# The 16 low-rank gate columns as one 32-column stationary operand

## The chip, the cores and the metric

One Trainium2 chip, one core. The metric is the device time of one execution in microseconds (us). Engines are called by their names in the profile: PE is TensorE, DVE is VectorE, ACT is ScalarE, POOL is GpSimd, SP issues most of the loads.

## What is computed

One layer of a hybrid decoder for 256 positions of width 2048, in float32: a mixer of three branches (S5, GLA, HGRN2) with a gated merge, then a squared-ReLU MLP, each followed by a layer norm. All branches read one projection `h = x @ w_in`, whose columns are split among them. The change concerns 16 of these columns, the low-rank input of GLA's decay gate:

```python
h = x @ w_in                                   # x 256 x 2048, w_in 2048 x 14352
(u_a, q_b, k_b, v_b, glow_b, gate_b, ...) = split_columns(h)      # glow_b: 16 columns

# GLA branch: per-key decay from the low-rank columns
log_a = log_sigmoid(glow_b @ w_gate + b_gate) / 16                # w_gate 16 x 512
o = chunk_gated_linear_attention(q_b * 128 ** -0.5, k_b, v_b, log_a)
```

## The kernel before

**Products in parts.** Weights and activations are float32. So that TensorE can run them in its faster 32-bit type (`F32R`), each is split into an upper part `hi` (a copy into F32R) and a lower part `lo` (the remainder), and products are summed without the lower-by-lower one. The columns of `x` are kept transposed as tiles `a` with 128 rows of the inner dimension, `a[0]` upper, `a[1]` lower (256 positions each), and `a[2]` both side by side (512 columns).

**Chunks and steps.** All weight matrices are worked off as a list of `Chunk`s. A chunk's weights come in pages of 512 KB, loaded on SP's queue 8 pages ahead (`fetch`, `emit_dma`) and split by ACT (`hi`, line 184) and DVE (`lo`, line 188) up to 6 steps ahead (`emit_split`, `emit_lower`). One pass of the loop at line 1288 is one step: half of a page's products. There are three kinds of chunk:

- "rows" (512 weight columns as the moving operand, activations stationary): three products of 512 columns for each 128 rows of the inner dimension, lines 1327 to 1329.
- "cols" (256 weight columns, 128 at a time as the stationary operand): for each 128 rows a product of 512 moving columns with `hi` against `a[2]` (line 1332) and one of 256 with `lo` against `a[0]` (line 1333), called a pair here. The result has two halves, which `joined` adds (ACT copies one, DVE adds it to the other).
- "low": one chunk alone, for the 16 low-rank columns. It is like "cols", with 128 weight columns of which only the first 16 are wanted: 2 pages, 4 steps, 16 pairs. Its evacuation `ev_low` (line 760) adds the two halves of 16 rows into `glT` and spawns `gla_decay`.

The order is: a "rows" chunk of v (16 steps), four "cols" chunks of the S5 input u (32 steps, 0 to 47 with v's), the "low" chunk (steps 48 to 51), two "cols" chunks for gK, two for gQ, and so on; then the other branches, the merge, the output projection and the MLP.

**Tasks.** Work that isn't a chunk's products runs as generators in `tasks`: at each step `run_tasks` advances those that are due. `yield n` makes a task due 2n steps later. Tasks of priority -1 always run; others only while an estimate of the work handed to DVE and ACT (`used`, reduced by 1240 ns each a step) is below zero, in order of priority. The S5 branch (`s5_params`, `s5_prepare`, `s5_main`) runs at priority 2 and 5 beside the chunks up to about 760 us: `s5_prepare` transposes blocks of S5 matrices on TensorE (lines 440 to 442), `s5_main` computes tables on POOL (lines 484 to 489), scans on DVE and small products on TensorE (lines 510 and 554). `gla_decay` (line 768, priority 0) loads the gate's weights on ACT's queue, multiplies (line 779, plain float32) and computes the decay `gA`; `gla` waits for `gA`, gQ and gK before it starts its attention.

Each engine works through its instructions in program order. Tiles of 512 KB ("pg", 41 of them) and of 256 KB ("hf", 18) are handed out and freed by the program; PSUM has three accumulators for chunks ("acc"), three tiles for tasks ("m") and two for S5 ("m2").

Of the kernel before, what the change touches and what calls it, by code (L numbers as in the profile page):

```python
# [8 lines left out]
F32 = mybir.dt.float32  # L9
F32R = mybir.dt.float32r  # L10
U8 = mybir.dt.uint8
AF = mybir.ActivationFunctionType
ALU = mybir.AluOpType
# [14 lines left out]
C_UA, C_QB, C_KB, C_VB, C_GL, C_GB = 0, 1024, 1536, 2048, 3072, 3088  # L28
# [8 lines left out]


class Chunk:

# [12 lines left out]
def trunk_kernel(ctx: ExitStack, tc, io, out):  # L56
    nc = tc.nc
    V, S, G, T = nc.vector, nc.scalar, nc.gpsimd, nc.tensor
# [25 lines left out]
    def half(shape=(128, 2, 256), dt=F32):  # L84
        return take("hf", shape, dt)

    def free(*tiles):
        for t in tiles:
            tag = "pg" if id(t) in live["pg"] else "hf"
            del live[tag][id(t)]  # L90

    def psm(shape=(128, 512)):
        uid[0] += 1
        return psa.tile(list(shape), F32, tag="m", bufs=NM, name=f"m{uid[0]}")
# [10 lines left out]
    def tt(o, a, b, op):  # L105
        used["v"] += size(o) / 0.96 + 80
        V.tensor_tensor(o, a, b, op=op)  # L107
# [12 lines left out]
    def act(o, a, f, bias=None, scale=None, accum=None):  # L120
        used["s"] += size(a) / 1.3 + 180
        kw = {}
        if bias is not None:
            kw["bias"] = bias
        if scale is not None:
            kw["scale"] = scale
        if accum is not None:
            kw["accum_out"] = accum
        S.activation(o, a, f, **kw)  # L129
# [11 lines left out]
    w_in = io["w_in"][0]  # L141
# [5 lines left out]
    chunks = []  # L147
# [53 lines left out]
    def spawn(gen, prio):  # L201
        tasks.append([prio, now[0], gen, len(tasks)])
        tasks.sort(key=lambda x: (x[0], x[3]))
# [529 lines left out]
    def ev_page(key, i, func=None, scale=None):  # L733

        def f(t, ps):
            n = 2 * i + t
            if n == 0:
                R[key] = page()
            o = R[key][:, n, :]
            joined(ps, o, scale)  # L740

            def later():
                yield 0.5
                if func is not None:
                    act(o, o, func)
                if n == 3:
                    yield 0.5
                    R[key, "ok"] = True
            spawn(later(), -1)
        return f  # L750
# [6 lines left out]
        while not all(k in R for k in keys):  # L757
            yield 1

    def ev_low(t, ps):  # L760

        glT, b = half((16, 256)), half((16, 256))
        act(b, ps[0:16, 256:512], AF.Copy)
        tt(glT, ps[0:16, 0:256], b, ALU.add)
        free(b)
        spawn(gla_decay(glT), 0)

    def gla_decay(glT):

        wg = half((16, 512))  # L770
        S.dma_start(wg, io["gla_w_gate"][0])
        yield 2
        A = page()
        L = page()
        for hp in range(2):
            ps = psm()
            for i in range(2):
                hd = 2 * hp + i
                T.matmul(ps[:, i * 256:(i + 1) * 256], lhsT=wg[:, hd * 128:(hd + 1) * 128], rhs=glT,
                         start=True, stop=True)  # L780
            for i in range(2):
                hd = 2 * hp + i
                act(A[:, hd, :], ps[:, i * 256:(i + 1) * 256], AF.Identity, bias=S5["bgate"][:, hd:hd + 1])
        free(wg, glT)
        yield
        act(L, A, AF.Abs)
        act(L, L, AF.Exp, scale=-1.0)
        yield 0
        act(L, L, AF.Ln, bias=1.0)
        stt(A, A, 0.0, L, ALU.min, ALU.subtract)  # L790
        yield
        act(A, A, AF.Exp, scale=1.0 / 16.0)
        free(L)
        R["gA"] = A

    def gla():
        yield from wait_for("gA", ("gQ", "ok"), ("gK", "ok"))
        nw = half((128, 256))
        S.dma_start(nw, io["gla_norm_w"].to_broadcast([128, 256]))
        ss = cst.tile([128, 2, 4], F32, name="gss")  # L800

        def sink(t, g, ps):
            y = R["gg", g][:, t, :]
            y3 = y.rearrange("p (h d) -> p h d", h=2)
            tt(y3, y3, nw.unsqueeze(1).to_broadcast([128, 2, 256]), ALU.mult)
            squares(ss[:, t, 2 * g:2 * g + 2], [ps[:, i * 256:(i + 1) * 256] for i in range(2)])
            tt(y, ps, y, ALU.mult)
            yield 0
        yield from attention(R["gQ"], R["gK"], R["gA"], [("gv", "ok"), ("gg", "ok")],
                             lambda t, h: R["gv", h // 2][:, t, (h % 2) * 256:(h % 2) * 256 + 256], 256, sink)  # L810
        free(nw)
        yield from rms(ss.rearrange("p a b -> p (a b)"), 256)
        for t in range(2):
            for h in range(4):
                y = R["gg", h // 2][:, t, (h % 2) * 256:(h % 2) * 256 + 256]
                ts(y, y, ss[:, t, h:h + 1], None, ALU.mult)
            yield 0
        free(R["gv", 0], R["gv", 1])
        R["yB"] = True
# [244 lines left out]
    xact = parts(xq)  # L1064
# [13 lines left out]
    def four(w, c0, ev):  # L1078
        return [col_chunk(w, D, c0 + 256 * i, xact, ev(i)) for i in range(2)]
# [18 lines left out]
    def at(chunk, f):  # L1098
        hooks.setdefault(id(chunk), []).append(f)
# [4 lines left out]
    v_chunk(0)  # L1104
    for c in range(2):
        four(w_in, C_UA + c * 512, lambda i: ev_u(c, i))
    chunks.append(Chunk([w_in[:, C_GL:C_GL + 128].rearrange("(kt p) n -> p kt n", p=128)], xact, ev_low, "low"))
    at(four(w_in, C_KB, lambda i: ev_page("gK", i))[0], lambda: spawn(gla(), 0))
    four(w_in, C_QB, lambda i: ev_page("gQ", i, scale=128 ** -0.5))
    v_chunk(1)  # L1110
    for c in range(2):
# [160 lines left out]
    def accumulator():  # L1272
        tags = [("acc", NACC)] * NACC + ([("m2", 2)] * 2 if "done" in S5 else [])
        tag, bufs = tags[acc_n[0] % len(tags)]
        acc_n[0] += 1
        uid[0] += 1
        return psa.tile([128, 512], F32, tag=tag, bufs=bufs, name=f"acc{uid[0]}")
# [10 lines left out]
    for s, (c, ku, j, t) in enumerate(steps):  # L1288
        now[0] = s
        if id(c) not in started:  # L1290
            started.add(id(c))
            for f in hooks.get(id(c), []):
                f()
        old = split_n[0]
        early = ln_from - 8 <= s < ln_from + 12
        kept = max(0, 8 - len(x1q)) if early and s >= ln_from else 0
        while (split_n[0] < len(order) and first_use[split_n[0]] <= s + (14 if early else 2 if s < 14 else LA + 4 * (s > 660))
               and len(live["pg"]) + 2 + kept <= limit["pg"]):
            emit_split()
        if early:  # L1300
            emit_lower(split_n[0])
        evacuate()
        fetch()
        run_tasks(1240, 1240)
        emit_lower(old if s >= 10 else split_n[0])
        if s < 14 and t == 1:
            x_piece(s // 2 + 1)
        k = c.index[ku, j]
        if k not in sps:
            emit_split()  # L1310
        emit_lower(k + 1)
        hi, lo = sps[k]
        kpu = c.kpu
        nk = len(c.units) * kpu
        if t not in c.ps:
            c.ps[t] = c.ps[0] if c.kind == "low" and t else accumulator()
        ps = c.ps[t]
        nj = kpu // 2
        wn = c.units[0].shape[2]
        wh, wl = (a.rearrange("p a b -> p (a b)").rearrange("p (k n) -> p k n", n=wn) for a in (hi, lo))  # L1320
        for i in range(nj):
            kt = ku * kpu + j * nj + i
            f, l = kt == 0, kt == nk - 1
            a = c.act(kt)
            if c.kind == "rows":
                sl = slice(t * 128, (t + 1) * 128)
                T.matmul(ps, lhsT=a[0][:, sl], rhs=wh[:, i, :], start=f, stop=False)  # L1327
                T.matmul(ps, lhsT=a[0][:, sl], rhs=wl[:, i, :], start=False, stop=False)  # L1328
                T.matmul(ps, lhsT=a[1][:, sl], rhs=wh[:, i, :], start=False, stop=l)  # L1329
            elif c.kind == "cols" or i // (nj // 2) == t:  # L1330
                n = slice(t * 128, (t + 1) * 128) if c.kind == "cols" else slice(0, 128)
                T.matmul(ps, lhsT=wh[:, i, n], rhs=a[2], start=f, stop=False)  # L1332
                T.matmul(ps[:, 0:256], lhsT=wl[:, i, n], rhs=a[0], start=False, stop=l)  # L1333
        uses_left[k] -= 1
        if uses_left[k] == 0:
            free(*sps.pop(k))
        if ku == len(c.units) - 1 and j == 1 and (c.kind != "low" or t == 1):
            done.append((c, t, ps))
    evacuate()
    guard = 0  # L1340
# [53 lines left out]
```

## Time and profile before

| | |
|---|---|
| median of 3 runs | 1694.68 us (1694.48 to 1695.0) |
| profiled execution | 1694.67 us, span 1692.9 us |
| PE busy | 1669.5 us (99%) |
| DVE busy | 1196.9 us (71%) |
| ACT busy | 826.0 us (49%) |
| POOL busy | 166.3 us (10%) |
| read from HBM | 308.71 MB |

The span is that of the recorded instructions; the execution's own time has 1.8 us more around it. PE's busy time counts products whose ends are modelled and overlap, so the distance between the starts of two products tells the pace, not the length of one. In lines of instructions the columns are start in us, length in us, engine, line of the kernel, operation, output and inputs, count, and in brackets the engine's idle time before and what ended it. PEld is the weight load, which runs beside products. Helpers record their line: L129 is every ACT activation, L107 every DVE operation on two tensors, L134 every transpose.

### The profile page before, as it was taken

Reading aid. Unit: us, or ns where it says so; the run is one execution under the profiler, and the core shown is the slowest. Engines: PE = TensorE matmul, PEld = TensorE weight load, DVE = VectorE, ACT = ScalarE, POOL = GpSimd, SP = SyncE. Lnnn points to the kernel's source line nnn. Section 1 sums busy time; section 2 is a strip of 40 time slices with the busy share of each in tenths; the row PEclk is TensorE's granted clock in tenths of the full one; section 3 lists DMA queues with packets and bytes.
Section 4 is the critical chain, followed back from the end, with each engine's and each line's share of the span. In section 5 each row is a group of like instructions: output and inputs, shape, how many; then the busy total and the mean of one; then the engine's idle time right before and its main releaser. Section 6 shows DMA issues by size and latency. Waiting matters only on the chain.

```text
span 1692.9 us, 24205 instructions
## 1 busy us (share of the span) xinstructions
PE 1669.5 (99%) x9390; PEld 1385.6 (82%) x9390; DVE 1196.9 (71%) x1586; ACT 826.0 (49%) x1166; POOL 166.3 (10%) x121
## 2 busy tenths in 40 slices
PE   8999999999999999999999999999999999999996
PEld 6888888887877877878888888888888888888885
DVE  5978889698999999985675667555455555555556
ACT  4463554464545444435554466454454545454540
POOL 3132211021322322100000000000000000000000
PEclk9999999999999999999999999999999999999998
DMA  9855565555555665766686555656656565656661
GB/s 289 255 160 170 166 178 173 159 166 163 173 179 150 222 188 165 244 199 196 189 278 210 171 162 157 196 178 191 199 187 210 168 207 166 219 173 203 205 216 50
DMA packets 222899, 318.70 MB, mean 188 GB/s; under 512 B 13204, under 2 KB 122128, under 8 KB 222784
## 3 DMA queue, kind: packets, MB, share of 16 engines
q1 hardware_dynamic: 218448, 309.45, 58.6%
q10 hardware_dynamic: 3568, 6.46, 1.3%
q0 software_dynamic: 768, 1.25, 0.5%
q8 instruction: 74, 1.21, 0.3%
q14 instruction: 41, 0.34, 0.1%
HBM read 308.71 MB, written 2.10 MB: 184 GB/s over the span
## 4 chain that ended last, share of the span: by engine, by line
PE 91%; DVE 5%; ACT 1%; DMA 1%; issue 1%; SPq 0%; DVEq 0%; ACTq 0%
PE acc L1332 21%; PE acc L1327 19%; PE acc L1328 19%; PE acc L1329 19%; PE acc L1333 10%; DVE pg L107 2%; DMA pg<-in_w_in_dram 1%; DVE hf L107 1%; PE m L554 1%; ACT pg L129 1%; PE m L134 1%; DVE pg L118 1%; ACT hf L129 1%; PE m L625 1%; PE pb L510 0%
## 5 line engine op out<-in xcount | busy, mean ns | idle before, releaser
L129 ACT ACTIVATE pg<-pg 128x1024 fp32r<-128x1024 f32 (+2 forms) x604 | 603.4, 1028 | 416.5 <-DVE pg L107 131.9
L107 DVE TENSOR_TENSOR pg<-pg,pg 128x1024 fp32r<-128x1024 f32 (+3 forms) x646 | 752.5, 1192 | 65.4 <-ACT pg L129 39.5
L1327 PE MATMUL acc<-pg,pg 128*128 128x512 f32 x1504 | 595.4, 396 | 4.2 <-ACT pg L129 3.6
L1328 PE MATMUL acc<-pg,pg 128*128 128x512 f32 x1504 | 587.7, 391 | 1.1 <-DVE pg L107 1.1
L1329 PE MATMUL acc<-pg,pg 128*128 128x512 f32 x1504 | 587.2, 390 | 0.3 <-DVE pg L107 0.2
L1332 PE MATMUL acc<-pg,pg 128*128 128x512 f32 x1552 | 551.2, 400 | 0.0
L1333 PE MATMUL acc<-pg,pg 128*128 128x256 f32 x1552 | 436.2, 281 | 0.0
L1332 PEld LDWEIGHTS acc<-pg,pg 128*128 128x128 f32 x1552 | 292.2, 188 | 72.4 <-issue 0.7
L1327 PEld LDWEIGHTS acc<-pg,pg 128*128 128x128 f32 x1504 | 282.9, 188 | 68.2 <-issue 5.4
L1329 PEld LDWEIGHTS acc<-pg,pg 128*128 128x128 f32 x1504 | 282.7, 188 | 61.1 <-DVE pg L107 1.1
L1328 PEld LDWEIGHTS acc<-pg,pg 128*128 128x128 f32 x1504 | 283.1, 188 | 59.5 <-DVE pg L107 4.0
L1333 PEld LDWEIGHTS acc<-pg,pg 128*128 128x128 f32 x1552 | 293.9, 189 | 0.7 <-DVE pg L107 0.2
L129 ACT ACTIVATE hf<-acc 128x256 f32<-128x256 f32 (+2 forms) x103 | 39.9, 387 | 186.1 <-PE acc L1333 177.7
L107 DVE TENSOR_TENSOR pg<-pg,acc 128x512 f32<-128x512 f32 x56 | 38.3, 684 | 123.0 <-PE acc L1329 123.0
L107 DVE TENSOR_TENSOR hf<-acc,hf 128x256 f32<-128x256 f32 (+1 forms) x69 | 29.1, 421 | 134.6 <-ACT hf L129 134.6
L107 DVE TENSOR_TENSOR hf<-hf,hf 128x512 f32<-128x512 f32 (+1 forms) x144 | 117.3, 833 | 3.5 <-ACT hf L129 1.4
L129 ACT ACTIVATE hf<-hf 128x256 f32<-128x256 f32 (+1 forms) x152 | 67.7, 455 | 2.1 <-DMA hf<-pg 0.2
L129 ACT ACTIVATE pg<-acc 128x512 f32<-128x512 f32 x40 | 23.8, 594 | 77.9 <-PE acc L1329 77.8
L107 DVE TENSOR_TENSOR hf<-pb,hf 128x256 f32<-128x256 f32 x128 | 46.4, 414 | 19.1 <-PE pb L510 13.3
L107 DVE TENSOR_TENSOR pg<-hf,pg 128x256 fp32r<-128x256 f32 x84 | 34.7, 422 | 27.7 <-ACT pg L129 27.6
L129 ACT ACTIVATE pg<-m 128x512 fp32r<-128x512 f32 (+2 forms) x35 | 19.7, 562 | 66.2 <-PE m L134 47.1
L484 POOL TENSOR_TENSOR hf<-pg 128x512 f32<-128x512 f32 x16 | 19.8, 1238 | 303.4 <-PE pb L510 85.9
(127 smaller groups left out, 665.9 us busy)
## 6 DMA issues: line engine op xcount, KB each, us to landing
pg<-in_w_in_dram SPq DMA_DIRECT2D x224, 512.0 KB, 4.2
pg<-in_w_mlp_in_dram SPq DMA_DIRECT2D x128, 512.0 KB, 4.6
pg<-in_w_mlp_out_dram SPq DMA_DIRECT2D x128, 512.0 KB, 4.1
pg<-in_w_up_dram SPq DMA_DIRECT2D x48, 512.0 KB, 4.7
pg<-in_w_out_dram SPq DMA_DIRECT2D x32, 512.0 KB, 5.1
pg<-in_s_w_glu_dram SPq DMA_DIRECT2D x8, 512.0 KB, 4.8
hf<-pg SPq DMA_DIRECT2D x96, 32.0 KB, 2.1
hf<-hf SPq DMA_DIRECT2D x96, 32.0 KB, 1.9
```

The lines of the kernel that those rows point to most:

```text
L107: V.tensor_tensor(o, a, b, op=op)
L118: V.scalar_tensor_tensor(o, a, s, b, op0=op0, op1=op1)
L129: S.activation(o, a, f, **kw)
L134: T.transpose(ps[:, i * 128:(i + 1) * 128], s, ident)
L484: G.tensor_tensor(co, coarse(cs), fine(cs), op=ALU.mult)
L554: T.matmul(yps[r, 0:256], lhsT=W[:, 2 + ri, r], rhs=m[:, i, :], start=ri == 0, stop=ri == 1)
L625: T.matmul(ps[32 * c:32 * c + 32, i * 16:(i + 1) * 16], lhsT=Kf[:, r], rhs=q4[:, :, 1, :], start=True, stop=True)
L1327: T.matmul(ps, lhsT=a[0][:, sl], rhs=wh[:, i, :], start=f, stop=False)
L1328: T.matmul(ps, lhsT=a[0][:, sl], rhs=wl[:, i, :], start=False, stop=False)
L1329: T.matmul(ps, lhsT=a[1][:, sl], rhs=wh[:, i, :], start=False, stop=l)
L1332: T.matmul(ps, lhsT=wh[:, i, n], rhs=a[2], start=f, stop=False)
L1333: T.matmul(ps[:, 0:256], lhsT=wl[:, i, n], rhs=a[0], start=False, stop=l)
```

## The change

The "low" chunk goes. A task `low_rank` of priority -1, spawned when gK's first chunk starts, loads only the 16 columns (64 bytes of each of 2048 rows) on POOL's queue, splits them into one tile with the upper part in columns 0 to 15 and the lower part in columns 16 to 31, and multiplies with that as a 32-column stationary operand against `a[2]`: 16 products of 512 moving columns. The 32 rows of the result are added over the two halves to `glT` with 32 rows, and the gate's weights are loaded twice, one copy below the other, so that the gate's product sums the upper and lower part.

```diff
-    def ev_low(t, ps):
-
-        glT, b = half((16, 256)), half((16, 256))
-        act(b, ps[0:16, 256:512], AF.Copy)
-        tt(glT, ps[0:16, 0:256], b, ALU.add)
-        free(b)
+    def low_rank():
+        wgr, wgl = half((128, 16, 16)), half((128, 16, 32), F32R)
+        G.dma_start(wgr, w_in[:, C_GL:C_GL + 16].rearrange("(kt p) n -> p kt n", p=128))
+        yield 4
+        act(wgl[:, :, 0:16], wgr, AF.Copy)
+        yield 0.5
+        tt(wgl[:, :, 16:32], wgr, wgl[:, :, 0:16].bitcast(F32), ALU.subtract)
+        yield 1
+        ps = psm()
+        for kt in range(16):
+            T.matmul(ps[0:32, :], lhsT=wgl[:, kt, :], rhs=xact(kt)[2], start=kt == 0, stop=kt == 15)
+        glT, b = half((32, 256)), half((32, 256))
+        act(b, ps[0:32, 256:512], AF.Copy)
+        yield 0.5
+        tt(glT, ps[0:32, 0:256], b, ALU.add)
+        free(b, wgr, wgl)
         spawn(gla_decay(glT), 0)
 
     def gla_decay(glT):
 
-        wg = half((16, 512))
-        S.dma_start(wg, io["gla_w_gate"][0])
+        wg = half((32, 512))
+        for i in range(2):
+            S.dma_start(wg[16 * i:16 * i + 16], io["gla_w_gate"][0])
...
-    chunks.append(Chunk([w_in[:, C_GL:C_GL + 128].rearrange("(kt p) n -> p kt n", p=128)], xact, ev_low, "low"))
-    at(four(w_in, C_KB, lambda i: ev_page("gK", i))[0], lambda: spawn(gla(), 0))
+    kb = four(w_in, C_KB, lambda i: ev_page("gK", i))
+    at(kb[0], lambda: spawn(gla(), 0))
+    at(kb[0], lambda: spawn(low_rank(), -1))
...
-            c.ps[t] = c.ps[0] if c.kind == "low" and t else accumulator()
+            c.ps[t] = accumulator()
...
-            elif c.kind == "cols" or i // (nj // 2) == t:
-                n = slice(t * 128, (t + 1) * 128) if c.kind == "cols" else slice(0, 128)
+            else:
+                n = slice(t * 128, (t + 1) * 128)
...
-        if ku == len(c.units) - 1 and j == 1 and (c.kind != "low" or t == 1):
+        if ku == len(c.units) - 1 and j == 1:
```

## The prediction

> **What bounds the kernel now.** I read the page first, then the stretches around the change, then the instructions themselves in order of time. The head of the page:
>
> ```profile
> span 1692.9 us, 24205 instructions
> PE 1669.5 (99%) x9390; PEld 1385.6 (82%) x9390; DVE 1196.9 (71%) x1586; ACT 826.0 (49%) x1166; POOL 166.3 (10%) x121
> PE 91%; DVE 5%; ACT 1%; DMA 1%; issue 1%; SPq 0%; DVEq 0%; ACTq 0%
> ```
>
> TensorE (PE) is busy for 99% of the span and carries 91% of the chain that ended last. So TensorE work that disappears comes off the time, unless something else is late at that place. The low-rank work lies near 85 to 91 us. From the table of stretches the row of 85 to 96 us (busy us of PE, PEld, DVE, ACT, POOL, then granted clock, DMA share, GB/s), the low-rank products in order of time on TensorE, and ScalarE's evacuations at both ends:
>
> ```profile
> 85.00:96.00 11.00, 8.98 (x51) 7.33 (x50) 10.95 (x14) 3.52 (x6) 7.51 (x6) 0.98 0.26 80
> 85.22 0.28 PE L1333 MATMUL acc<-pg,pg 128*128 128x256 f32 x1
> 85.34 0.40 PE L1332 MATMUL acc<-pg,pg 128*128 128x512 f32 x1
> ...
> 90.99 0.40 PE L1332 MATMUL acc<-pg,pg 128*128 128x512 f32 x1
> 85.54 0.38 ACT L129 ACTIVATE hf<-acc 128x256 f32<-128x256 f32 x1
> ...
> 91.19 0.38 ACT L129 ACTIVATE hf<-acc 16x256 f32<-16x256 f32 x1 [3.37 <-PE acc L1333]
> ```
>
> The 16-partition evacuation at 91.19 is that of the low-rank chunk, the 128-partition one at 85.54 that of the chunk before. So the chunk's 16 pairs of products run from 85.34 to 90.99, gap-free, one pair per 0.353 us. Behind them comes a wait:
>
> ```profile
> 92.38 0.28 PE L1333 MATMUL acc<-pg,pg 128*128 128x256 f32 x1
> 93.75 0.44 PE L134 MATMUL m<-ident,s5eb 128*128 128x128 f32 x2 [1.09 <-DVE s5eb L435]
> 95.12 0.44 PE L134 MATMUL m<-ident,s5ec 128*128 128x128 f32 x2 [0.94 <-DVE s5ec L112]
> ```
>
> Here TensorE waits for VectorE (DVE), which is busy for 10.95 of 11 us, as it prepares the S5 operands.
>
> **The change part by part.** *Products removed.* 16 pairs, 90.99 - 85.34 = 5.65 us, all on TensorE's path.
>
> *Products added.* 16 products with a 32-column stationary operand and 512 moving columns, none of which the trace has in this form. Rows that come near: 512-column products back to back with 128 stationary columns, and 32-column stationary operands in plain f32 (output of the S5 branch), two interleaved column groups of four products each:
>
> ```profile
> 745.42 0.39 PE L1327 MATMUL acc<-pg,pg 128*128 128x512 f32 x1
> ...
> 746.10 0.39 PE L1327 MATMUL acc<-pg,pg 128*128 128x512 f32 x1
> 206.46 0.39 PE L1329 MATMUL acc<-pg,pg 128*128 128x512 f32 x1
> 206.77 1.06 PE L554 MATMUL m<-hf,hf 128*32 128x256 f32 x8
> 207.77 0.50 PE L1327 MATMUL acc<-pg,pg 128*128 128x512 f32 x1
> L554 PEld LDWEIGHTS m<-hf,hf x128: 106/110/110, 146.2 to 756.9; 128*32 128x32 f32 x128
> L554 PE MATMUL m<-hf,hf x128: 379/379/404, 146.2 to 757.1; 128*32 128x256 f32 x128
> ```
>
> The first rows are three products apart, (746.10 - 745.42)/3 = 0.227 us per 512 columns. I take that: 16 x 0.227 = 3.63 us. The 32-column rows give the same pace: from first to last of one group's four products, (1.06 - 0.379)/3 = 0.227 us. The weight loads of 0.110 us do not add to it, so they are hidden behind the product before. Going from 128- to 32-column operands costs 206.77 - 206.46 = 0.31 us instead of 0.227, and about the same on the way back (207.83 - 0.379 = 207.45 to 207.77): 0.08 us each, 0.16 us together. Ends: 3.63 us without the two changes; 16 x (0.227 + 0.110) + 0.16 = 5.55 us if every weight load shows. Near the lower end, because the nearest form (32 columns) hides its loads. Taken: 3.8 us.
>
> *The position.* The new products stand at step 59 (spawned at 48, then 8 + 1 + 2 steps of yields), inside the gK chunks. The wait at 93 us stays: the S5 transposes are emitted at step 53 by yields that nothing removed here feeds, and five steps of 1.41 us stand in front of them from 85.34 on in either kernel. Until then VectorE has the same splits to do, one page per two steps in either. Cost 0.
>
> *Splits and loads removed.* Two 512 KB loads on SP's queue, two page splits on ScalarE (ACT) and VectorE:
>
> ```profile
> L129 ACT ACTIVATE pg<-pg 128x1024 fp32r<-128x1024 f32 x569 | 584.4, 1054 | 392.9 <-DVE pg L107 124.7 <-PE acc L1328 119.9 <-PE acc L1329 96.5
> L107 DVE TENSOR_TENSOR pg<-pg,pg 128x1024 fp32r<-128x1024 f32 x569 | 700.8, 1255 | 39.1 <-ACT pg L129 33.8 <-PE acc L1328 2.9 <-issue 0.9
> L129 ACT ACTIVATE hf<-hf 128x256 f32<-128x256 f32 x120 | 49.4, 412 | 1.9
> L107 DVE TENSOR_TENSOR hf<-acc,hf 128x256 f32<-128x256 f32 x68 | 28.6, 421 | 134.6 <-ACT hf L129 134.6
> L771 ACTq DMA_DIRECT2D hf<-in_gla_w_gate_dram x1: 397/397/397, 91.2 to 91.2; - x1
> 108.70 0.42 DVE L107 TENSOR_TENSOR pg<-acc,hf 128x256 f32<-128x256 f32 x1 [7.64 <-ACT hf L129]
> ```
>
> ScalarE loses 2 x 1.05 and gains 0.41 (first part of the 256-element split) and 0.40 (issue of the second gate-weight load); VectorE loses 2 x 1.26 and gains 0.42. None of it is on the path: the new evacuations replace equal ones. I count nothing for 1.7 us of VectorE work saved, because VectorE then idles 7.64 us before 108.70 and carries no debt onwards. In the other direction the cover of the new split is three steps (56 to 59, about 4 us), against 0.41 + 0.42 us of work; without it TensorE would wait those 0.8 us.
>
> *Chain behind it.* The gate decay starts at step 60 instead of 52. Its readers wait for gQ as well, whose chunks end at step 80, twenty steps later. No wait is added there.
>
> *The new load.* It is issued from POOL's queue, 2048 runs of 64 bytes. In program order it stands ahead of the S5 tables (priority -1 at step 48; the tables follow at 51), and only 11 of the 18 half tiles were handed out before, so it need not wait for a buffer. POOL idles from 16.3 us. So it goes out at about 16.3 us, into the crowded start:
>
> ```profile
> 10.04 1.71 POOL L291 DMA_DIRECT2D pg<-in_s_b_re_dram  x1 [0.18 <-issue]
> 11.74 1.69 POOL L292 DMA_DIRECT2D pg<-in_s_b_im_dram  x1
> 15.72 0.55 POOL L587 DMA_DIRECT2D dg<-in_c_diag_dram  x1
> 79.49 1.43 POOL L484 TENSOR_TENSOR hf<-pg 128x512 f32<-128x512 f32 x1 [63.23 <-DVE pg L114]
> pg<-in_w_in_dram SPq DMA_DIRECT2D x224, 512.0 KB, 4.2
> pg<-in_s_b_re_dram POOLq DMA_DIRECT2D x1, 256.0 KB, 9.8
> pg<-in_s_b_im_dram POOLq DMA_DIRECT2D x1, 256.0 KB, 10.8
> dg<-in_c_diag_dram POOLq DMA_DIRECT2D x1, 16.0 KB, 10.1
> 10.71 15.86 DMA pg<-in_w_in_dram
> ```
>
> The nearest rows are the S5 matrices, 4096 runs of 64 bytes each: they land at 19.8 and 22.5 us, 2.7 us apart, so 2048 runs take about 1.4 us of the DMA engines. POOL's earlier loads land until 15.72 + 10.1 = 25.8 us, so this one moves after that. The weight page that holds up the path, with 15.86 us to landing instead of the usual 4.2, is in at 26.57, mostly ahead of it; later pages may slip by 1.4 us. Ends: 0 (the later pages have slack) and 1.4 us. Taken: 0.3 us, since only the page after the critical one is tight.
>
> *Drift.* S5 work goes by step numbers, the chunks come 4 steps earlier, so in the DVE-heavy stretch to 760 us other pieces meet. What TensorE there waits for VectorE is little:
>
> ```profile
> PEld acc L1328 <- DVE pg L107: 4.0, 8, 0.8
> ```
>
> I count 0 and give it 1.6 us to either side, less than half of these 4.0 us (8 waits, the longest 0.8).
>
> Sum: -5.65 + 3.8 + 0.3 = -1.55 us. The profiled execution took 1694.67 us (its span of 1692.9 and 1.8 around it), the median of the runs shown is 1694.68; so 1694.67 - 1.55 = **1693.1 us**. That is 0.09%, under the 0.2% (3.4 us) that a measurement of this kernel can tell from no change.
>
> **The rivals.** *Weight loads show.* All 16 stationary operands fill the same rows and the same 32 columns. If a load had to wait until the product before is through, the products would cost 5.55 us and the time would be 1694.67 - 5.65 + 5.55 + 0.3 = 1694.9. Against it: the 0.227 us step of the 32-column rows, which use the same columns in succession. The Trainium skill, "TensorE: Matmul & The Clock Gate", Part 3 (packing small matmuls), "The mechanism", states in its list of what overlaps that a weight load does so only when the row group differs; by that rule none would be hidden here. The trace's 0.227 us step disagrees.
>
> *Slower: products in four passes.* If the 32-column form is not run at the single-pass rate, it costs like the plain f32 gate products:
>
> ```profile
> 101.26 1.99 PE L779 MATMUL m<-hf,hf 16*128 16x256 f32 x8
> 103.18 0.50 PE L1332 MATMUL acc<-pg,pg 128*128 128x512 f32 x1
> ```
>
> Four products of 256 columns in 103.18 - 101.26 = 1.92 us, so 0.96 us per 512 columns, 15.4 us for 16: 1694.67 - 5.65 + 15.4 + 0.3 = 1704.7. It decides above (5.65 + 3.4)/16 = 0.57 us per product. Against it: both operands are of the same type as in L1327, which runs at 0.227. The Trainium skill, "FP8 and Floating Point Precision", section "TensorE Precision Notes", gives true FP32 four passes; the 0.96 against 0.227 us agrees with that.
>
> *Drift becomes a gain.* If most of the DVE waits quoted last, or the wait at 93 us (1.37 us between 92.38 and 93.75, 1.37 more to 95.12), falls away, 2.5 us more go: 1690.6. For it only that other pieces meet; against it, that the wait at 93 us hangs on work wholly ahead of the change.
>
> **How the numbers follow.** Forecast, PE-bound saving of about 1.5 us with its own range of 1691.5 to 1694.7: 0.73. Weight loads show: 0.10. Four passes, or the new load holding up the start by over 5 us: 0.04. Drift gain: 0.10. Drift loss of 2 to 4 us, still within 0.2% (1695 to 1697): 0.03. The range of 1691.2 to 1695.2 holds the forecast, the weight-load case and part of the drift. Faster by over 0.2% means under 1691.3: the drift gain and a tail of the forecast, 0.12. Slower by over 0.2%, over 1698.1: 0.04. Within: 0.84.
>
> **What would show it.** In the changed kernel 16 products of 32 columns near 105 us, 0.227 us apart (0.34: weight loads; 0.96: four passes); two pages fewer among the splits; the gap-free pairs from UA to gK without the chunk; the same TensorE wait near 93 us; POOL's new load near 16 us and landings of weight pages between 26 and 32 us later by at most 1.4. Wrong if TensorE waits for that load's split, or if waits for VectorE between 110 and 760 us change by more than 2 us.

## The result and the profile after

The changed kernel took 1705.15 us (median of 4 runs, 1704.19 to 1706.62), the kernel before beside it 1694.58 us: a ratio of 1.0067, 95% interval 1.0054 to 1.0079. It is slower by 10.6 us, where 1.55 us less were predicted. The profiled execution took 1704.19 us. The head of its page, and the chain that ended last:

```profile
span 1702.4 us, 24172 instructions
PE 1670.3 (98%) x9374; PEld 1383.2 (81%) x9374; DVE 1195.0 (70%) x1585; ACT 825.7 (48%) x1166; POOL 167.6 (10%) x122
PE 84%; DVE 9%; issue 2%; ACT 2%; DMA 2%; SPq 0%; DVEq 0%
```

The busy times hardly differ from before. The chain does: PE carries 84% of it instead of 91%, DVE 9% instead of 5%. So the time is in waits for DVE, not in the new products. The changed stretch, in order of time on TensorE (line numbers of the changed kernel; L1347 and L1348 are the pair, L773 the low-rank product, L133 a transpose):

```profile
86.53 0.40 PE L1347 MATMUL acc<-pg,pg 128*128 128x512 f32 x1
...
94.00 0.38 PE L133 MATMUL m<-ident,s5eb 128*128 128x128 f32 x2
94.21 0.38 PE L133 MATMUL m<-ident,s5ec 128*128 128x128 f32 x2
...
102.90 3.86 PE L773 MATMUL m<-pg,hf 128*32 128x512 f32 x16
106.60 0.40 PE L1347 MATMUL acc<-pg,pg 128*128 128x512 f32 x1
```

The 16 products take 106.60 - 102.90 = 3.70 us to the next start, 0.23 us each. gK's first product has come forward from 90.99 to 86.53, and the S5 transposes no longer wait. Everything so far is a gain. Then come waits that the kernel before did not have:

```profile
30.96 0.50 PE L1342 MATMUL acc<-pg,pg 128*128 128x512 f32 x1 [2.71 <-ACT pg L128]
129.78 0.50 PE L1347 MATMUL acc<-pg,pg 128*128 128x512 f32 x1 [0.86 <-DVE pg L117]
151.48 0.74 PE L624 MATMUL m<-pg,pg 128*32 128x16 f32 x64 [3.73 <-DVE pg L106]
508.98 0.50 PE L1342 MATMUL acc<-pg,pg 128*128 128x512 f32 x1 [1.01 <-DVE pg L106]
545.71 0.50 PE L1342 MATMUL acc<-pg,pg 128*128 128x512 f32 x1 [1.32 <-DVE pg L106]
574.68 0.50 PE L1343 MATMUL acc<-pg,pg 128*128 128x512 f32 x1 [0.41 <-DVE pg L106]
639.93 0.50 PE L1343 MATMUL acc<-pg,pg 128*128 128x512 f32 x1 [1.86 <-DVE pg L106]
```

A wait also costs time behind itself. The table of stretches (columns as in the prediction; the clock is the third number from the end) has one behind the wait of 93 us in the kernel before:

```profile
95.30:98.50 3.20, 3.20 (x12) 2.73 (x12) 3.20 (x4) 2.49 (x3) 0.76 (x1) 0.52 0.10 26
```

and two in the changed kernel, behind the waits at 151 and 640 us, with the stretch behind the wait at 545 us for comparison:

```profile
152.70:156.10 3.40, 3.40 (x9) 2.64 (x8) 3.40 (x6) 1.06 (x1) 0.00 (x0) 0.51 0.56 159
545.00:550.00 5.00, 4.29 (x24) 3.07 (x24) 4.96 (x8) 1.85 (x3) 0.00 (x0) 1.00 0.62 190
640.70:644.10 3.40, 3.40 (x10) 2.58 (x9) 3.37 (x5) 1.82 (x3) 0.00 (x0) 0.52 0.00 0
```

For some 3.3 us the granted clock is 0.52, which costs 1.6 us on top of the wait in these executions (the last section has the same waits without it); behind the 1.32 us at 545 us it stays at 1.00.

The 7584 products of chunks that both kernels have in common stand in the same order, so the start of the same product in both traces tells where the time went:

| same product, before to after (us) | offset | what lies between this row and the last |
|---|---|---|
| 29.8 to 31.0 | +1.2 | longer wait for ACT in the start |
| 91.0 to 86.5 | -4.5 | 16 pairs gone (-5.65) |
| 103.2 to 92.6 | -10.6 | wait at 93 us and its slow clock gone (-3.9); gate product (1.9) and four transposes (0.3) now later |
| 113.2 to 106.6 | -6.6 | the 16 new products; the four transposes |
| 133.2 to 129.8 | -3.4 | gate product; wait at 130 us |
| 193.1 to 195.4 | +2.3 | wait at 151 us and its slow clock |
| 504.2 to 506.7 | +2.5 | |
| 575.2 to 580.4 | +5.2 | waits at 509, 543 (0.42), 545 and 575 us, less one of 0.59 in the kernel before |
| 641.3 to 650.0 | +8.7 | wait at 640 us and its slow clock |
| last | +9.3 | |

(From 133 us on the rows are taken where as many products of tasks lie behind as at the end. Between them the offset swings by up to 2.6 us, as S5 products stand before or behind the product compared.) So after 113 us some 14 us are lost beside the gate product's 1.9, of them 3.3 by the slow clock. What follows asks why.

### The profile page after: what moved, and what is told of

It is laid out like the page before. It is cut to its first block, busy times and chain, and to the rows that moved or that the text cites. A ratio compares the mean times of both kernels' runs of the same rounds, so it can differ in the third digit from the quotient of the medians.

```text
span 1702.4 us, 24172 instructions
## 1 busy us (share of the span) xinstructions
PE 1670.3 (98%) x9374; PEld 1383.2 (81%) x9374; DVE 1195.0 (70%) x1585; ACT 825.7 (48%) x1166; POOL 167.6 (10%) x122
## 4 chain that ended last, share of the span: by engine, by line
PE 84%; DVE 9%; issue 2%; ACT 2%; DMA 2%; SPq 0%; DVEq 0%
PE acc L1347 19%; PE acc L1342 18%; PE acc L1343 17%; PE acc L1344 17%; PE acc L1348 10%; DVE pg L106 4%; DVE hf L106 2%; DMA pg<-in_w_in_dram 1%; ACT pg L128 1%; DVE pg L117 1%; DVE hf L533 1%; PE m L553 1%; PE m L133 1%; PE m L624 1%; ACT hf L128 1%
## 5 line engine op out<-in xcount | busy, mean ns | idle before, releaser
L128 ACT ACTIVATE pg<-pg 128x1024 fp32r<-128x1024 f32 (+3 forms) x602 | 601.7, 1028 | 436.2 <-PE acc L1343 148.7
L106 DVE TENSOR_TENSOR pg<-pg,pg 128x1024 fp32r<-128x1024 f32 (+4 forms) x644 | 753.0, 1196 | 64.2 <-ACT pg L128 38.7
L1347 PE MATMUL acc<-pg,pg 128*128 128x512 f32 x1536 | 544.8, 399 | 1.2 <-DVE pg L117 0.9
L1348 PE MATMUL acc<-pg,pg 128*128 128x256 f32 x1536 | 431.0, 281 | 0.0
L1347 PEld LDWEIGHTS acc<-pg,pg 128*128 128x128 f32 x1536 | 288.5, 188 | 73.4 <-DVE pg L117 1.2
L1348 PEld LDWEIGHTS acc<-pg,pg 128*128 128x128 f32 x1536 | 290.1, 189 | 0.6
L128 ACT ACTIVATE hf<-acc 128x256 f32<-128x256 f32 (+1 forms) x102 | 39.6, 388 | 180.3 <-PE acc L1348 172.0
L106 DVE TENSOR_TENSOR hf<-acc,hf 128x256 f32<-128x256 f32 x68 | 28.7, 422 | 137.0 <-ACT hf L128 137.0
L106 DVE TENSOR_TENSOR hf<-hf,hf 128x512 f32<-128x512 f32 (+2 forms) x145 | 109.9, 776 | 1.9
L128 ACT ACTIVATE hf<-hf 128x256 f32<-128x256 f32 (+2 forms) x153 | 68.1, 455 | 2.1
```

## The experiments

Theory A: the new form costs nothing; the tasks stand at other places among the chunks, and S5's work on DVE meets other work. A1, later: what makes such a meeting expensive is POOL's table work running beside DVE; against it A2, that DVE's own load makes it so. Rivals: B, the 32-column products or their result cost it; C, the new load in the start does, with a debt that is carried on.

**The 32 columns in place.** Chunk, pages and steps of the kernel before are kept; the lower parts go into columns 16 to 31 of the upper tile, and 16 products replace the pairs.

```diff
+    tt(h8[:, :, 16:32], r8[:, :, 0:16], h8[:, :, 0:16].bitcast(F32), ALU.subtract)
-    T.matmul(ps, lhsT=wh[:, i, n], rhs=a[2], start=f, stop=False)
-    T.matmul(ps[:, 0:256], lhsT=wl[:, i, n], rhs=a[0], start=False, stop=l)
+    T.matmul(ps[0:32, :], lhsT=wh[:, i, 0:32], rhs=a[2], start=f, stop=l)
```

> The kernel before with its four low-rank steps, pages and tasks kept where they are; only the products are changed: the lower parts of the 16 columns are written into columns 16 to 31 of the upper part's tile, and each of the 16 pairs becomes one product with a 32-column stationary operand. Every task is handed out at the same step as before. Theory A (the new products are as cheap as predicted, and the loss comes from the order of the tasks against the chunks): 16 products at 0.24 us instead of 16 pairs at 0.353, so 1694.6 - 1.8 = 1692.8 us, and no new waits after 110 us. Rival B (something in the 32-column form itself, its products, its operand or its 32-row result, brings the loss): 1700 us or more.

Measured: 1694.12 us (11 runs) against 1693.97, ratio 0.9999 (0.9990 to 1.0008). Its products on TensorE, in order of time:

```profile
85.23 3.86 PE L1346 MATMUL acc<-pg,pg 128*32 128x512 f32 x16
88.93 0.40 PE L1343 MATMUL acc<-pg,pg 128*128 128x512 f32 x1
90.19 0.39 PE L1344 MATMUL acc<-pg,pg 128*128 128x256 f32 x1 [0.86 <-DVE pg L107]
...
92.72 0.44 PE L134 MATMUL m<-ident,s5eb 128*128 128x128 f32 x2 [1.09 <-DVE s5eb L445]
```

B falls: the same 3.86 us, no loss. But the medians show no gain either. In the trace the products save 1.9 us; then a split is late by 0.86 us as soon as TensorE is ahead, and the wait at 93 us is as long as before. (The execution shown is the fastest of the 11, and its clock behind that wait stayed at 1.00.) So DVE takes back part of what TensorE gains here; whether the rest reaches the time isn't resolved.

**Order alone.** The kernel before with its old pairs; during the four steps of the "low" chunk no task advances, and the gate's decay is delayed, so that the tasks stand among the other chunks as in the changed kernel.

```diff
-        now[0] = s
+        now[0] = min(s, 48) if c.kind == "low" else s - 4 * (s > 51)
-        run_tasks(1240, 1240)
+        if c.kind != "low":
+            run_tasks(1240, 1240)
```

> The kernel before with its old low-rank pairs, but the tasks are held during the four low-rank steps, and the gate decay starts as late as in the changed kernel, so that every later task stands at the same place among the chunks as in the changed kernel. No 32-column product, no new load. Theory A (order): the loss is there without the change: 1705.1 + 1.8 for the old products - 1.2 for the start that is not held up = 1705.7 us (1702 to 1709), with waits of TensorE of over 1 us near 150, 545 and 640 us. Rival B (32-column form) and rival C (the new load at the start, from which all else follows): 1694 to 1696 us.

Measured: 1706.21 us (4 runs), ratio 1.0071 (1.0057 to 1.0084). Its waits on TensorE:

```profile
131.90 0.50 PE L1347 MATMUL acc<-pg,pg 128*128 128x512 f32 x1 [0.85 <-DVE pg L118]
153.59 0.73 PE L625 MATMUL m<-pg,pg 128*32 128x16 f32 x64 [3.75 <-DVE pg L107]
511.11 0.50 PE L1342 MATMUL acc<-pg,pg 128*128 128x512 f32 x1 [1.02 <-DVE pg L107]
547.84 0.50 PE L1342 MATMUL acc<-pg,pg 128*128 128x512 f32 x1 [1.31 <-DVE pg L107]
642.05 0.54 PE L1343 MATMUL acc<-pg,pg 128*128 128x512 f32 x1 [1.86 <-DVE pg L107]
```

These are the waits of the changed kernel, 2.1 us later and within 0.02 us as long (one of 0.71 us at 100 us is its own). The order of the tasks alone makes them, with no 32-column product and no new load in the program. A is shown.

**The load later.** The changed kernel with the new load behind the first S5 tables in POOL's queue (`yield 2` ahead of the `dma_start` and 2 behind it, instead of 4 behind).

> The changed kernel, but the load of the 16 columns is issued two yields later, so that it stands behind the first S5 tables in POOL's queue and goes out near 89 us instead of 16 us. All tasks stay at their steps. Theory A (order): the first 0.5 MB pages come as before, TensorE's gap at 28 us shrinks from 3.1 to 1.6 us, and 1.2 us are won at the start; the later waits stay: 1704 us (1703 to 1705.5). Rival C (the start is the cause): 1692 to 1695 us.

Measured: 1702.55 us (4 runs), ratio 1.0051 (1.0036 to 1.0067). The wait in the start is 1.49 us instead of 2.71; the waits from 150 us on are unchanged (3.74, 1.02, 1.32, 1.86). So there is no debt that is carried on from the start, and C falls as the cause of the loss. By the traces this version gains 1.1 us in the start, and 1.7 us more because its clock stayed at 1.00 behind the 1.86 us; the medians, which were not measured side by side, are 2.6 us apart. That the load itself made the start longer isn't shown, see the experiments with the POOL copy below.

**Half the lag.** Tasks held in two of the four steps only.

> The kernel before with the tasks held during two of the four low-rank steps (the last two), all products old. It puts the S5 and attention tasks two steps later among the chunks instead of four. Theory A in the form 'any other meeting of pieces costs or saves by chance': a time anywhere from 1692 to 1706, not in proportion. Theory A in the form 'the later the S5 work, the worse': half of the held kernel's loss, near 1700 us. Rivals B and C: 1694.6 us.

Measured: 1695.95 us (10 runs), ratio 1.0014 (1.0005 to 1.0023). It has waits of its own (0.73 us at 119, 0.80 at 149, 1.25 at 208), and behind 500 us those of the kernel before. The loss doesn't grow in step with the lag; it depends on which pieces meet.

**Less POOL work.** In both kernels, four of the six table instructions of `s5_tables` are left out (only the first factors of cosine and sine stay, so the tables are incomplete).

```diff
         G.tensor_tensor(co, coarse(cs), fine(cs), op=ALU.mult)
-        G.tensor_tensor(w, coarse(sn), fine(sn), op=ALU.mult)
-        G.tensor_tensor(co, co, w, op=ALU.subtract)
         G.tensor_tensor(so, coarse(sn), fine(cs), op=ALU.mult)
-        G.tensor_tensor(w, coarse(cs), fine(sn), op=ALU.mult)
-        G.tensor_tensor(so, so, w, op=ALU.add)
```

The kernel before:

> The kernel before, with four of the six POOL instructions of each S5 table left out (the tables then hold one product each instead of a sum of two, so the S5 branch's values are not meant). All tasks stay at their steps. It serves as the base for the next kernel: POOL's table work falls from 152 to about 50 us, and VectorE's instructions, which take 1.2 to 1.9 us beside POOL and 0.7 to 1.2 us alone, get shorter. Both theories: the waits at 93, 285, 504 and 531 us shrink, 1690 us (1688 to 1692.5).

The changed kernel:

> The changed kernel with the same four POOL instructions left out. Theory A1 (the new order costs time because POOL's tables now slow VectorE's instructions where TensorE is about to wait): with little POOL work the loss is gone, within 2 us of the kernel before treated alike, so 1688 to 1693 us. Theory A2 (the new order bunches VectorE's own work, POOL plays no part): the waits near 150, 545 and 640 us stay, 7 us or more above the kernel before treated alike: 1697 us or more.

Measured, beside 1694.13 us: before with less POOL work 1686.07 us (4 runs; 0.9950, 0.9937 to 0.9964), changed with less POOL work 1689.49 us (6 runs; 0.9973, 0.9962 to 0.9984). The first gained 4 us more than expected. The gap between the two orders falls from 10.6 to 3.4 us: less than the 7 that A2 asked for, but more than the 2 of A1. The stretch of 340 to 740 us of the kernel before, the changed one, and the kernel before with less POOL work:

```profile
340.00:740.00 400.00, 398.59 (x2286) 321.98 (x2286) 368.48 (x502) 189.47 (x246) 94.20 (x61) 1.00 0.61 187
```
```profile
340.00:740.00 400.00, 394.30 (x2254) 316.95 (x2253) 369.13 (x504) 189.23 (x246) 102.97 (x67) 1.00 0.59 184
```
```profile
340.00:740.00 400.00, 400.00 (x2291) 324.35 (x2290) 340.44 (x505) 192.00 (x241) 25.87 (x21) 1.00 0.60 187
```

DVE does the same number of instructions (502, 504, 505) in 368, 369 and 340 us: each is shorter without POOL beside it. In this stretch DVE is busy as long in the order before as in the changed one, so the orders differ in where its work meets POOL's, not in how much it is. With 28 us less of DVE work TensorE never idles in 400 us, and with it DVE is at 92%. These two runs therefore don't separate A1 from A2 in full: without POOL's work DVE has more room in the whole stretch, not only where TensorE is about to wait. In the changed kernel with less POOL work all waits for DVE behind 150 us are gone; 0.67 us at 130, 0.22 and 0.50 at 145 to 149 and the longer start stay.

**Gate decay not delayed.** As "order alone", without the delay of the decay: another order up to about 165 us, from there that of the changed kernel.

> The kernel before with the tasks held during the four low-rank steps, but without the delay of the gate decay: the order of the tasks differs from the changed kernel's in the first part (up to about 165 us) and is the same from there on. If each wait comes from the order around it: the waits near 131 and 153 us are gone or other ones, those near 511, 547, 577 and 642 us stay, 1694 + 7 = 1701 us (1699 to 1703). If the late waits are a debt carried from the first part: 1694 to 1696 us.

Measured: 1702.3 us (4 runs, 1698.5 to 1704.44), ratio 1.0052 (1.0036 to 1.0067). The wait at 131 us is gone, the one at 150 us is 3.11, and the late ones are the same (1.01, 1.31, 1.86). So they don't hang on the wait at 131 us, nor on how long the one at 150 us is; the order without any wait there wasn't run. The profiled execution is the fastest of the four, and its clock stayed at 1.00 behind all these waits.

**POOL held off at 93 us.** One small POOL copy that reads the last S5 operand stands ahead of the second S5 tables, so that POOL begins them only when DVE has copied those operands; first on the version with 32 columns in place, then on the kernel before, then both on one chip.

```diff
                 yield from room("hf", 3, 4)
+                if hb == 0:
+                    G.tensor_copy(behind, S5["EC"][:, 1, 1, 63:64])
                 s5_tables(hb + 1)
```

32 columns in place:

> The kernel with the new products in place, and one copy of one column on POOL ahead of the second S5 tables, which reads the last S5 operand that VectorE prepares for the transposes near 93 us. POOL's tables then wait for these instructions instead of running beside them. Theory A1 (POOL beside VectorE makes the wait at 93 us): the four instructions take 0.3 instead of 1.0 us each, TensorE's two waits of 1.0 us each and part of the slow clock behind them go, and the saved products show: 1690 us (1689 to 1692). Theory A2: 1693 to 1694.5, no change against the kernel before.

The kernel before:

> The kernel before, unchanged but for one small POOL copy that reads the last S5 operand (s5ec) ahead of the second S5 tables, so that POOL computes them only after the S5 operands are copied. If the wait of the S5 transposes near 93 us comes from POOL running beside DVE (theory), the two waits of 1.09 and 0.94 us there go and the time is about 2 us under the kernel before: 1692. If DVE's own load makes it (rival: 10.95 of 11 us busy there, and before has 0.83 us more of split work than the version with 32 columns in place), the waits stay within 0.3 us and so does the time: 1694.

32 columns in place, again:

> The low-rank products with 32 columns in place, with the same POOL copy, on the same chip as the kernel before with the copy alone. If what the 32 columns save (5.65 - 3.86 = 1.8 us) reaches the time once the S5 transposes do not wait, this is about 1.5 us under the other: 1690.5 to 1691.3. If the saving is taken back elsewhere (rival), both are equal within 0.5 us.

Measured: 32 columns in place 1691.26 us (11 runs; 0.9984, 0.9975 to 0.9993), and on the other chip 1690.70 (11 runs; 0.9981, 0.9972 to 0.9990) beside the kernel before with the copy alone, 1691.51 (11 runs; 0.9983, 0.9974 to 0.9992). DVE in the kernel before, in order of time:

```profile
91.61 1.09 DVE L112 TENSOR_SCALAR s5ec<-pg,gmask 128x128 f32<-128x128 f32 x1
92.72 1.07 DVE L435 COPY s5eb<-pg 64x64 f32<-64x64 f32 x2
93.83 1.23 DVE L112 TENSOR_SCALAR s5ec<-pg,gmask 128x128 f32<-128x128 f32 x1
```

with POOL's second tables beside it,

```profile
91.57 1.06 POOL L484 TENSOR_TENSOR hf<-pg 128x512 f32<-128x512 f32 x1 [2.31 <-DVE pg L107]
92.59 1.05 POOL L485 TENSOR_TENSOR hf<-pg 128x512 f32<-128x512 f32 x1
93.72 1.26 POOL L486 TENSOR_TENSOR hf<-hf,hf 128x512 f32<-128x512 f32 x1
```

and DVE with the POOL copy, where these tables begin at 94.90:

```profile
92.86 0.27 DVE L112 TENSOR_SCALAR s5ec<-pg,gmask 128x128 f32<-128x128 f32 x1
93.14 0.30 DVE L435 COPY s5eb<-pg 64x64 f32<-64x64 f32 x2
93.47 0.29 DVE L112 TENSOR_SCALAR s5ec<-pg,gmask 128x128 f32<-128x128 f32 x1
```

The same copies are four times as long beside POOL, and that was the whole wait at 93 us: without it the time falls by 2.9 us. By the start of the same product 4.0 us are won between 92 and 103 us (the 2.03 us of idle time, the 1.6 us of slow clock, and 0.4), and 1.2 of them are lost ahead of it, in the start. What the 32 columns add to this is 0.8 us between the medians, but the runs overlap (1690.43 to 1692.23 against 1691.35 to 1691.68), so it is not resolved; in the trace a split late by 0.87 us takes back part of their 1.9. Both versions are faster than the kernel before and than the changed one.

That loss in the start bears on the new load. The latest weight page, from issue to landing, in the changed kernel and in the kernel before with the POOL copy:

```profile
10.70 17.06 DMA pg<-in_w_in_dram
```
```profile
10.73 17.07 DMA pg<-in_w_in_dram
```

The second has no new load, and its one added instruction runs at 94 us. Yet its page takes as long as that of the changed kernel; in the kernel before it took 15.86 us. The first product behind it starts at 31.0 to 31.1 us in all five versions with either the load at 16 us or the POOL copy, and at 29.7 to 30.1 in the seven others. What makes the start longer is open; the load is not the only thing that can.

## Why the prediction was wrong

**Products removed and added: right.** -5.65 us is in the table of offsets, and the new products took 3.86 us (3.8 predicted). "Weight loads show" would have been 0.34 us a product and is out. "Four passes" gave 1704.7 us, almost the time measured, by a mechanism that did not occur: 0.23 us a product, not 0.96. A time that fits a rival is no evidence for it until its place in the trace is looked up.

**New load: its cost is open.** It went out where predicted and landed 10.9 us later. Issue and landing in the changed kernel:

```profile
16.27 1.20 POOL L765 DMA_DIRECT2D hf<-in_w_in_dram  x1
hf<-in_w_in_dram POOLq DMA_DIRECT2D x1, 128.0 KB, 10.9
```

The term was 0.3 us, bounded by 1.4. The start of the same product is 1.2 us later, and the latest weight page landed at 27.76, not mostly ahead of the load. But the kernel before with the POOL copy has the same later start without the load, so no run shows how much of the 1.2 us is the load's.

**Position and the wait at 93 us: wrong.** "The wait at 93 us stays", since it hangs on DVE work ahead of the change. The instructions are indeed the same. Their lengths were not: POOL's second tables began at 91.57 in the kernel before, amid the copies, and at 98.37 in the changed one. This gave 3.9 us that the forecast did not have.

**Drift: the step that failed.** It was sized 0, give or take 1.6 us, from the 4.0 us of waits that the kernel before had (one row of the weight loads' waits, over the whole execution). Measured, it was about 14 us behind 113 us, and the order alone gave +12 us. By the traces the terms are -5.65 + 3.70 for the products, +1.2 in the start, -3.9 at 93 us and +14 of drift, +9.3 together. A sum of existing waits bounds what can be won, not what can be lost. The prediction's own test shows it: TensorE's waits for DVE from 110 to 760 us rose from 2.4 to 11.1 us, not by under 2. The row that would have warned is that of 340 to 740 us: DVE at 92% with splits at most six steps (8.5 us) ahead has little to pay any new meeting with. The rival that ends slower was then sought in the products, where the trace spoke against it, and the loss by drift got a chance of 0.03.

What a meeting looks like: DVE in the changed kernel ahead of the wait at 640 us,

```profile
628.65 1.27 DVE L533 TENSOR_TENSOR_SCAN hf<-p,hf 128x256 f32<-128x256 f32 x2
629.83 1.20 DVE L106 TENSOR_TENSOR pg<-pg,pg 128x1024 fp32r<-128x1024 f32 x1
631.06 1.40 DVE L106 TENSOR_TENSOR hf<-hf,hf 32x512 fp32r<-32x512 f32 x2
632.49 1.97 DVE L106 TENSOR_TENSOR pg<-pg,pg 128x1024 fp32r<-128x1024 f32 x1
634.38 3.18 DVE L533 TENSOR_TENSOR_SCAN hf<-p,hf 128x256 f32<-128x256 f32 x2
```

and POOL beside it:

```profile
631.82 1.55 POOL L486 TENSOR_TENSOR hf<-pg,pg 128x512 f32<-128x512 f32 x1 [10.42 <-DVE hf L106]
633.34 2.04 POOL L487 TENSOR_TENSOR hf<-pg,pg 128x512 f32<-128x512 f32 x1
635.46 1.55 POOL L488 TENSOR_TENSOR hf<-hf,hf 128x512 f32<-128x512 f32 x1
```

Two scans take 1.27 us alone and 3.18 with POOL, a split 1.20 and 1.97: 2.7 us lost, and the split that TensorE needs next is late by 1.86. In the kernel before the same scans, near 625 us, took 3.17 us and no product waited. So POOL's tables are not enough by themselves. That what DVE still owes at that moment decides, and that the order changes this, fits both traces but was not measured by itself.

**What stays open.** Of the 3.4 us that remain with less POOL work, 1.4 to 2.5 arise in the start by the traces (a slow clock of 3.4 us there included); the rest, near 130 and 145 to 149 us, wasn't taken apart. The wait at 130 us has no POOL instruction beside it: between 120 and 131 us POOL does nothing in the changed kernel. What else than POOL makes the wait of 3.73 us at 151 us was not tried by itself; with less POOL work 0.50 us of it is left.

## What to carry to other kernels

Where a second engine is nearly full, as DVE here at 92% of a stretch, moving its tasks by a few steps can cost more than the products saved (here 14 us against 1.95), so bound such a move by how far ahead that engine works, not by the waits seen now. Make a change of form in place first, without moving anything, and measure the order by itself. A wait for DVE whose length looks too long for its instructions may be another engine's work beside it; one small instruction that makes that engine wait was worth 2.9 us here, more than the whole change promised.

## What the runs showed of the hardware

The rows fit DVE and POOL taking turns. In those near 632 us the split issued at 632.49 fits POOL's L486 ending at 633.37 and 1.1 to 1.2 us of its own behind it; L487 then fits 1.0 us of waiting and 1.06 us of work, and each scan of 0.64 us fits about 1.0 us of waiting first. Splits that lie wholly beside POOL's tables take 1.90 us on average against 1.22 alone (25 of them in the changed kernel), while DVE operations with one operand in PSUM (128x256) take 0.41 against 0.42. The Trainium skill, "SBUF — State Buffer", "Who interferes with whom", says this of DVE instructions with two inputs in SBUF beside a GpSimd instruction that reads SBUF: the later one stops until the other is through. The trace agrees. That rule bore on this change, since the diff moves POOL's tables against DVE's work, and the prediction did not weigh it.

A wait of TensorE can cost nearly twice its length, but it doesn't in every execution. Behind the waits of 1.86 and 3.73 us in the changed kernel, and behind the two of 1.09 and 0.94 us close together in the kernel before, the granted clock was 0.51 to 0.52 for 3.2 to 3.4 us, and products of 512 columns came 0.43 us apart instead of 0.23. Waits of the same length were also met without it: 1.09 and 0.94 us with the 32 columns in place, 1.86 with the load later, 3.11 and 1.86 with the gate decay not delayed. The stretches behind the first and the second of these:

```profile
92.70:96.10 3.40, 2.44 (x14) 2.02 (x15) 3.37 (x4) 1.53 (x3) 1.26 (x1) 1.00 0.00 0
```
```profile
638.60:642.00 3.40, 3.33 (x14) 2.74 (x15) 3.37 (x6) 2.91 (x4) 0.00 (x0) 1.00 0.00 0
```

Behind the 2.71 us at 31 us in the changed kernel the clock was 1.00 too, and 0.50 for 3.4 us behind 2.38 us at the same place in the changed kernel with less POOL work. So the length of a wait alone doesn't settle it, and what does is open. Each kernel has one profile, and the slow stretch is worth 1.6 us, so a difference of that size between two traces should not be put down to the kernels.
